# One set of group-norm statistics for both halves of a retention head, applied a few quarter products later

## The chip, the core and the metric

One NeuronCore of a Trainium2 chip runs the whole layer. The engines are PE (TensorE, matmuls and transposes through the array), DVE (VectorE), ACT (ScalarE), POOL (GpSimd) and SP, which here issues the DMAs. The metric is the device time of one execution in microseconds, as a median of several runs; lower is better.

## What is computed

A decoder layer with two groups of eight heads of 128 channels over 1024 tokens: stick-breaking attention in group A, retention in group B. One input projection (2048 to 8192) feeds both and one output projection (2048 to 2048) takes both. Of the reference, what bears on the change:

```python
def head_group_norm(o, gain):
    mu = jnp.mean(o, axis=-1, keepdims=True)
    var = jnp.mean(jnp.square(o - mu), axis=-1, keepdims=True)
    return merge_heads((o - mu) * lax.rsqrt(var + EPS)) * gain.astype(jnp.float32)
...
    qr = rotary(split_heads(q_r, RET_HEADS))
    kr = rotary(split_heads(k_r, RET_HEADS)) * (HEAD_DIM ** -0.5)
    vr = split_heads(v_r, RET_HEADS).astype(jnp.float32)
    ob = head_group_norm(chunkwise_retention(qr, kr, vr), ret_norm_gain[layer])
    ob = ob * jax.nn.silu(z_r.astype(jnp.float32))
    y = jnp.concatenate([oa, ob], axis=-1).astype(x.dtype) @ w_out[layer]
```

`chunkwise_retention` works in eight chunks of 128 tokens: inside a chunk masked scores times values, across chunks a state of 128 x 128 that decays and grows. Each token's 128 outputs of a head are then normalized to mean 0 and variance 1.

## The kernel before

**The large products.** Both projections are matrix products split by a scheme with seven products in place of eight (P1 to P7 per group of 256 output columns). Each product runs four quarters (`j` from 0 to 3), and a quarter is three matmuls of 128x128 by 128x512 (`mm3`, L150 to L152): a weight's high part times a high part, high times low, low times high. In `run` (L357) the order of products in a group's steady state is P1, P4 and P3 of the group before, P6, P7, P2, P5. After each quarter `tick` (L168) runs. The unit of time in this text is therefore the quarter product.

**What a product needs.** For each, `first` (L256) makes the high part `wh` of its weights on ACT and `second` (L262) the low part `wl` on DVE, two products ahead; three buffers of each turn. `make` (L249) forms sums of weights on POOL. Behind products, `copied` (L279) takes a result out of PSUM on ACT, `added` (L290) adds one on DVE, and `copied` lets POOL add an older partial sum six quarters later (L287). Results then pass through rotary tables or a sigmoid (`second_put`, L804: L821 and L824, L841 to L849).

**The heads ride along.** The order on every engine is the program's own. `heads` is a generator: `yield n` lets n quarters go by. `at(k, fn)` (L165) puts work k quarters later; `tick` emits what is due. So an engine meets the work of a head between that of the products, and a waiting instruction holds up everything behind it on its engine.

**A retention head** (`ret_heads`, L1055) has two halves g of four chunks each. With T the quarter at which `values_r(0)` is called:

- at T and T + 6, `values_r(g)` (L1114) issues eight matmuls (seven in the first chunk's half) into `op`, a PSUM bank: A0 for the first half, C for the second. It allocates `on` (a `be` tile) and issues a DMA for `z`.
- one quarter after each, `stats` (L1127): four `bn_stats` on DVE;
- two after, `first_guess` (L1131): four `bn_aggr`, then `m` = variance + EPS and a first `y` for its inverse root;
- three, four and five after, `better` (L1137): one Newton step of three instructions each, on tiles of 128x4; the last also makes `m` = -mean times `y`;
- seven after, that is T + 7 and T + 13, `normal` (L1142): four ACT instructions that write `op` times `y` plus `m` into `on`.
- At T + 12 the next head's values are transposed on PE into banks A1 and B, where that head's inputs are there; ACT copies them to `v` at T + 14 (L755).
- At T + 18 and T + 20, `finish(g)` (L1153) transposes `on` on PE into bank B for the first half and A0 for the second, and one quarter later DVE multiplies by gain and gate (L1159).

In the trace `on` and `kd` are `be`, `pT` is `a`, `st6` is `st`, and q and k of the head are `r`.

## Time and profile before

| | us |
|---|---|
| median of 3 runs | 2088.36 |
| lowest and highest | 2084.07, 2092.07 |
| the profiled execution, whole | 2088.51 |
| its span, first to last instruction | 2086.7 |
| its mean granted PE clock (share of full speed) | 0.978 |
| `bn_stats` of the retention heads, first to last start | 1454.1 to 1827.0 |

A row of the timeline gives start and duration in us from the span's start, the engine, the source line, the operation, output and inputs, shapes, the count of instructions merged, and in brackets how long the engine was idle just before and what released it. A group's row gives the count, then busy us and the mean ns of one, then the idle time before. A row of waits gives who waited for whom, then us in total, times and the longest. Matmuls overlap: one takes 0.4 us from start to end, and the next starts about 0.23 us after it.

### The profile page before, as it was taken

The numbers are of one execution on the slowest core, as the hardware profiler recorded it, in microseconds if no ns is written. First come the engines' busy times: TensorE is split into PE (matmuls) and PEld (weight loads), VectorE is DVE, ScalarE is ACT, GpSimd is POOL, SyncE is SP. The second block draws the span as 40 slices with busy tenths as digits, with TensorE's granted clock in tenths as the row PEclk, the third lists the DMA queues.
The fourth block names the chain that finished last, engine by engine and source line by source line (L and its number), as shares of the span: only waits on it lengthen the run. The fifth ranks groups of instructions, "written<-read, shape, count | busy, mean of one in ns | idle before, by whom it ended". The sixth has DMA issues, their size and how long they took to land. (4 is left out here: it accounts for less than half of the span.)

```text
span 2086.7 us, 27289 instructions
## 1 busy us (share of the span) xinstructions
PE 1961.6 (94%) x9089; PEld 1565.1 (75%) x9089; DVE 1449.8 (69%) x2194; ACT 940.8 (45%) x1718; POOL 919.8 (44%) x627
## 2 busy tenths in 40 slices
PE   5879999998999999999999999899899988998998
PEld 4467777775767777788888888687787876887887
DVE  6678877566668576775766655888687877548555
ACT  4443344544455545554444544454353545335222
POOL 0434577765544335232222322777364654145443
PEclk9879999999999999999999999999999999999999
DMA  9748877533455454544434424777485876447665
GB/s 299 226 130 281 255 231 255 166 106 120 148 162 156 142 148 152 157 142 132 147 126 126 152 97 155 243 237 261 151 273 193 274 249 229 155 164 237 202 192 177
DMA packets 287330, 388.45 MB, mean 186 GB/s; under 512 B 32106, under 2 KB 164276, under 8 KB 287188
## 3 DMA queue, kind: packets, MB, share of 16 engines
q1 hardware_dynamic: 286784, 386.65, 57.4%
q8 instruction: 72, 1.18, 0.2%
q14 instruction: 70, 0.57, 0.1%
q10 hardware_dynamic: 404, 0.05, 0.0%
HBM read 278.51 MB, written 108.10 MB: 185 GB/s over the span
## 5 line engine op out<-in xcount | busy, mean ns | idle before, releaser
L264 DVE TENSOR_TENSOR wl_e_P<-wr_e,wh_e_P 128x512 fp32r<-128x512 f32 x560 | 528.4, 944 | 211.8 <-ACT wh_e_P L259 206.3
L254 POOL TENSOR_TENSOR wr_e<-wr_e,wr_e 128x512 f32<-128x512 f32 x240 | 352.8, 1485 | 494.7 <-DVE wl_e_P L264 441.0
L259 ACT ACTIVATE wh_e_P<-wr_e 128x512 fp32r<-128x512 f32 x560 | 350.1, 628 | 253.1 <-PE b_o L151 23.5
L254 POOL TENSOR_TENSOR wr_e<-wr_e 128x512 f32<-128x512 f32 x80 | 112.9, 1411 | 134.4 <-DVE wl_e_P L264 120.3
L915 DVE TENSOR_TENSOR_SCAN om<-om 128x128 f32<-128x128 f32 (+2 forms) x96 | 119.4, 1243 | 57.0 <-ACT om L906 55.2
L287 POOL TENSOR_TENSOR u_e<-u_e,c_e 128x512 f32<-128x512 f32 x50 | 78.2, 1567 | 119.8 <-DMA c_e<-part 84.5
L287 POOL TENSOR_TENSOR p_e<-p_e,c_e 128x512 f32<-128x512 f32 x49 | 73.5, 1500 | 112.4 <-DMA c_e<-part 70.4
L435 DVE SCALAR_TENSOR_TENSOR acc_b<-ada_b,silu_c,acc_b 128x512 f32<-128x512 f32 x88 | 97.5, 1108 | 29.5 <-DMA ada_b<-in_w_ada_dram 28.8
L152 PE MATMUL b_h<-S_h,wl_e_P 128*128 128x512 f32 x192 | 77.3, 402 | 11.8 <-DVE wl_e_P L264 11.8
L152 PE MATMUL b_e<-S_h,wl_e_P 128*128 128x512 f32 x192 | 77.3, 403 | 8.1 <-DVE wl_e_P L264 8.1
L150 PE MATMUL b_e<-S_h,wh_e_P 128*128 128x512 f32 x192 | 76.8, 400 | 5.7 <-ACT p_e L284 5.7
L921 DVE TENSOR_TENSOR be<-be,om 128x127 f32<-128x127 f32 (+2 forms) x96 | 75.0, 781 | 7.8
L151 PE MATMUL b_h<-S_l,wh_e_P 128*128 128x512 f32 x192 | 76.3, 398 | 2.4 <-DVE S_l L147 1.7
L150 PE MATMUL b_h<-S_h,wh_e_P 128*128 128x512 f32 x192 | 77.9, 406 | 0.0
L962 PE MATMUL oT<-a,v 128*128 128x256 f32 x320 | 76.9, 379 | 0.0
L150 PE MATMUL b_f<-S_h,wh_e_P 128*128 128x512 f32 x192 | 76.5, 398 | 0.0
L151 PE MATMUL b_e<-S_l,wh_e_P 128*128 128x512 f32 x192 | 76.0, 396 | 0.0
L150 PE MATMUL b_g<-S_h,wh_e_P 128*128 128x512 f32 x192 | 75.7, 394 | 0.0
L152 PE MATMUL b_f<-S_h,wl_e_P 128*128 128x512 f32 x192 | 75.1, 391 | 0.4 <-DVE wl_e_P L264 0.4
L151 PE MATMUL b_f<-S_l,wh_e_P 128*128 128x512 f32 x192 | 75.3, 392 | 0.0
L152 PE MATMUL b_g<-S_h,wl_e_P 128*128 128x512 f32 x192 | 75.1, 391 | 0.0
L151 PE MATMUL b_g<-S_l,wh_e_P 128*128 128x512 f32 x192 | 75.0, 391 | 0.0
(487 smaller groups left out, 5532.6 us busy)
## 6 DMA issues: line engine op xcount, KB each, us to landing
wr_e<-in_w_in_dram SPq DMA_DIRECT2D x128, 512.0 KB, 5.2
ada_b<-in_w_ada_dram SPq DMA_DIRECT2D x128, 256.0 KB, 4.8
c_e<-part SPq DMA_DIRECT2D x128, 256.0 KB, 4.9
ada_a<-in_w_ada_dram SPq DMA_DIRECT2D x64, 256.0 KB, 4.5
wr_e<-in_w_out_dram SPq DMA_DIRECT2D x32, 512.0 KB, 4.6
ld<-fin SPq DMA_DIRECT2D x54, 256.0 KB, 4.9
part<-p_e SPq DMA_DIRECT2D x48, 256.0 KB, 4.8
part<-u_e SPq DMA_DIRECT2D x48, 256.0 KB, 2.1
```

What stands on the lines that cost most here:

```text
L150: nc.tensor.matmul(o, a_hi, b_hi, start=first, stop=False, skip_group_check=True)
L151: nc.tensor.matmul(o, a_hi, b_lo, start=False, stop=False, skip_group_check=True)
L152: nc.tensor.matmul(o, a_lo, b_hi, start=False, stop=last, skip_group_check=True)
L254: nc.gpsimd.tensor_tensor(t[o], t[a], t[b], op=op)
L259: nc.scalar.activation(hi, self.t[RIGHT[p]], AF.Copy)
L264: nc.vector.tensor_tensor(lo, self.t[RIGHT[p]], self.parts[p].bitcast(F32), op=ALU.subtract)
L287: at(6, lambda: nc.gpsimd.tensor_tensor(t, t, o, op=ALU.add))
L435: nc.vector.scalar_tensor_tensor(acc, src, cj, acc, op0=ALU.mult, op1=ALU.add)
L915: nc.vector.tensor_tensor_scan(rev, rev, rev, init, op0=ALU.mult, op1=ALU.bypass)
L921: nc.vector.tensor_tensor(be[:, :m], be[:, :m], om[:, 1:m + 1], op=ALU.mult)
L962: nc.tensor.matmul(ob, v[:, j, :], a[:, cl], start=diag and ib == 0 and b == 0 and j2 == 0, stop=ch == 0 and ib == 2, skip_group_check=True)
```

## The change

`first_guess` and `better` are no longer run for each half. `stats` of both halves write into one `st6` of eight blocks. After the second half's `stats`, `first_guess` aggregates all eight, and the inverse root is worked out once on tiles of 128x8. From the second half's call, T + 6, the times are two, three, four and five quarters as before; `normal(0)` comes after eight (T + 14, before: T + 7) and `normal(1)` after ten (T + 16, before: T + 13). Each head's tiles `st6`, `mv`, `m`, `y`, `u` have one buffer of twice the size in place of two.

```diff
-            kds, pTs = {}, {}
+            kds, pTs, ops = {}, {}, {}
+
+            st6 = hs.tile([P, NB, 6], F32, tag="st6", bufs=1, name=f"st6_{h}")
+            mv = hs.tile([P, NB, 2], F32, tag="mv", bufs=1, name=f"mv_{h}")
+            m, y, u = (hs.tile([P, NB], F32, tag=f"{n}4", bufs=1, name=f"{n}4_{h}") for n in "myu")
...
-                st6 = hs.tile([P, 4, 6], F32, tag="st6", bufs=2, name=f"st6_{h}_{g}")
-                mv = hs.tile([P, 4, 2], F32, tag="mv", bufs=2, name=f"mv_{h}_{g}")
-                m, y, u = (hs.tile([P, 4], F32, tag=f"{n}4", bufs=2, name=f"{n}4_{h}_{g}") for n in "myu")
                 on = ht("be", f"on{g}")
+                ops[g] = op, on
 
                 def stats():
                     for j in range(4):
-                        nc.vector.bn_stats(st6[:, j, :], op[:, j, :])
+                        nc.vector.bn_stats(st6[:, 4 * g + j, :], op[:, j, :])
 
                 def first_guess():
-                    for j in range(4):
+                    for j in range(NB):
                         nc.vector.bn_aggr(mv[:, j, :], st6[:, j, :])
...
-                def normal():
+                def normal(g_):
+                    op_, on_ = ops.pop(g_)
                     for j in range(4):
-                        nc.scalar.activation(on[:, j, :], op[:, j, :], AF.Identity, scale=y[:, j:j + 1],
-                                             bias=m[:, j:j + 1])
-                for n, fn in ((1, stats), (2, first_guess), (3, better), (4, better), (5, lambda: better(True)),
-                              (7, normal)):
-                    at(n, fn)
+                        c_ = 4 * g_ + j
+                        nc.scalar.activation(on_[:, j, :], op_[:, j, :], AF.Identity, scale=y[:, c_:c_ + 1],
+                                             bias=m[:, c_:c_ + 1])
+                at(1, stats)
+                if g:
+                    for n, fn in ((2, first_guess), (3, better), (4, better), (5, lambda: better(True)),
+                                  (8, lambda: normal(0)), (10, lambda: normal(1))):
+                        at(n, fn)
```

## The prediction

> **What bounds the kernel now.** First the page's span and busy times.

> ```profile
> span 2086.7 us, 27289 instructions
> PE 1961.6 (94%) x9089; PEld 1565.1 (75%) x9089; DVE 1449.8 (69%) x2194; ACT 940.8 (45%) x1718; POOL 919.8 (44%) x627
> ```

> PE works nearly always, and the change leaves every matmul in place. It can pay only where PE waits, so next I read who waited for whom among 1440 and 1845 us, where the retention heads run.

> ```profile
> PE b_h L152 <- DVE wl_e_P L264: 11.6, 6, 3.0
> PE otp L1156 <- ACT v L755: 5.5, 3, 1.9
> ACT be L1144 <- DVE m L1140: 41.1, 13, 6.0
> ```

> The columns are us in total, times, longest. PE waits for the low parts of weights (`wl`, made on DVE) and, at `finish`, for ACT. ACT itself stands 41.1 us in front of `normal` until DVE has made `m`. The chain of statistics thus holds two engines back, and PE behind them. Where, the busy time by stretch shows: one row a head, 0 to 7, from the first product of `values_r(0)` to the last transpose of `finish(1)` (stretch, its us, busy us of PE, PEld, DVE, ACT, POOL with counts, granted clock, DMA share, GB/s).

> ```profile
> 1449.40:1477.93 28.53, 21.85 (x108) 17.92 (x107) 23.18 (x59) 10.31 (x21) 11.76 (x9) 0.89 0.69 217
> 1500.20:1518.30 18.10, 18.10 (x100) 15.57 (x99) 15.16 (x51) 8.24 (x18) 5.17 (x4) 1.00 0.41 132
> 1555.82:1582.00 26.18, 21.11 (x108) 17.01 (x107) 22.89 (x59) 10.30 (x21) 12.20 (x9) 0.93 0.62 209
> 1604.00:1622.10 18.10, 18.10 (x100) 15.57 (x99) 16.54 (x52) 8.42 (x18) 7.39 (x6) 1.00 0.58 184
> 1659.74:1687.37 27.63, 22.87 (x108) 18.63 (x107) 22.79 (x59) 10.30 (x21) 12.12 (x9) 0.88 0.74 244
> 1709.40:1736.80 27.40, 21.08 (x100) 16.31 (x99) 22.31 (x63) 13.64 (x28) 8.78 (x7) 0.94 0.70 222
> 1777.70:1796.70 19.00, 19.00 (x108) 16.37 (x107) 13.65 (x48) 8.77 (x18) 4.84 (x4) 1.00 0.46 151
> 1818.70:1836.80 18.10, 18.10 (x100) 15.57 (x99) 12.33 (x48) 8.26 (x17) 3.84 (x3) 1.00 0.35 116
> ```

> Heads 0, 2, 4 and 6 issue the same 108 matmuls there (eight transposes of the next head's `v` among them), and head 6 needs 19.00 us without a wait. So heads 0, 2 and 4 lose 9.53 + 7.18 + 8.63 = **25.3 us**. Of the heads with 100 matmuls, 1, 3 and 7 lose nothing against 18.10 and head 5 loses 9.3. Part of each loss is a clock of 0.5 that is granted after the waits, as in head 4:

> ```profile
> 1676.50:1679.90 3.40, 3.40 (x9) 2.67 (x9) 3.02 (x16) 0.37 (x1) 1.56 (x1) 0.50 0.56 176
> ```

> At half speed about half of such a stretch is lost; less the waits inside it I count 1.6 us.

> **What is removed on DVE.** The groups of that stage (busy us, mean ns | idle before):

> ```profile
> L143 DVE SCALAR_TENSOR_TENSOR y<-u,y 128x4 f32<-128x4 f32 x48 | 18.9, 394 | 1.6
> L141 DVE TENSOR_TENSOR u<-y 128x4 f32<-128x4 f32 x48 | 13.1, 273 | 1.2
> L142 DVE SCALAR_TENSOR_TENSOR u<-u,m 128x4 f32<-128x4 f32 x48 | 12.0, 250 | 1.7
> L1134 DVE TENSOR_SCALAR m<-mv 128x4 f32<-128x4 f32 x16 | 5.7, 353 | 0.5
> L139 DVE TENSOR_SCALAR y<-m 128x4 int32<-128x4 int32 x16 | 3.8, 236 | 0.6
> L1140 DVE SCALAR_TENSOR_TENSOR m<-mv,y 128x4 f32<-128x4 f32 x16 | 2.6, 162 | 0.6
> L141 DVE TENSOR_TENSOR nu<-ny x24: 174/176/1134, 541.6 to 878.2; 128x16 f32<-128x16 f32 x24
> ```

> These are 192 instructions, 56.1 us; half go, 12 a head, 96 in all. The others get eight columns: between the 0.16 us of four and the 0.176 us median of sixteen (last row), so at most 96 x 0.015 = 1.4 us more. The saving on DVE is between 96 x 0.16 = 15 us, at the unhindered price, and 28 us, at the mean. The 16 `bn_stats` and `bn_aggr` of a head stay; four `bn_aggr` move into the later chain (0.37 us, below). What this is worth depends on where DVE is late, so I walk through two heads.

> **Heads 0, 2 and 4.** Their order is the same; head 2 from its timeline (start, us):

> ```profile
> 1561.97 0.37 DVE L1133 BATCH_NORM_AGGREGATE mv<-st 128x2 f32<-128x6 f32 x4
> 1565.98 1.24 DVE L141 TENSOR_TENSOR u<-y 128x4 f32<-128x4 f32 x1
> 1567.26 1.20 DVE L142 SCALAR_TENSOR_TENSOR u<-u,m 128x4 f32<-128x4 f32 x1
> 1568.49 1.21 DVE L143 SCALAR_TENSOR_TENSOR y<-u,y 128x4 f32<-128x4 f32 x1
> 1571.81 0.67 DVE L264 TENSOR_TENSOR wl_e_P<-wr_e,wh_e_P 128x512 fp32r<-128x512 f32 x1
> 1576.27 0.16 DVE L1140 SCALAR_TENSOR_TENSOR m<-mv,y 128x4 f32<-128x4 f32 x1
> 1565.54 2.91 POOL L254 TENSOR_TENSOR wr_e<-wr_e,wr_e 128x512 f32<-128x512 f32 x2 [0.70 <-DVE wl_e_P L264]
> 1570.52 1.51 ACT L1144 ACTIVATE be<-op,m,y 128x128 f32<-128x128 f32 x4 [5.98 <-DVE m L1140]
> 1578.37 1.09 ACT L755 ACTIVATE v<-vtp_vT 128x512 f32<-128x512 f32 x2
> 1572.54 0.50 PE L152 MATMUL b_h<-S_h,wl_e_P 128*128 128x512 f32 x1 [2.95 <-DVE wl_e_P L264]
> 1579.52 0.66 PE L1156 MATMUL otp<-ident,be 128*128 128x128 f32 x4 [1.75 <-ACT v L755]
> 1794.28 0.60 PE L1156 MATMUL otp<-ident,be 128*128 128x128 f32 x4
> ```

> The first chain spreads from 1561.97 to 1570.5, where `normal(0)` is released, because POOL is at work and three of its instructions take 1.2 us. `wl` at 1571.81 stands behind it, and PE for 2.95 us. Two full-width instructions of 0.67 us are mixed in; the other 7.2 us go. `wl` can move up to about 1564.6, and this wait of PE is gone. The one chain left has 12 instructions of 0.2 us (0.16, and 6.2 us of idle before 192 of them, 0.03 each), 2.4 us, and eight `bn_aggr`, 0.74 us. Today's second chain ends at 1576.4 and lasts 2.8 us at these prices, so it would begin at 1573.6 - 7.2 = 1566.4 at the earliest; the two full-width instructions ahead of it then meet POOL's burst (two sums of 1.45 us) and may be held up a microsecond each, so 1568.4 at the latest. I take 1567.9, nearer the late end because POOL's burst itself depends on a `wl` and comes earlier too. One instruction of the chain I count as held up, by 1.05 us (1.21 - 0.16). `m` then ends near 1572.1.

> PE's side: head 6 goes from 1777.70 to `finish(0)` at 1794.28, 16.58 us; added to 1555.82 that is 1572.4 unhindered. The next product's `wl` follows `m`: 1572.1 + 0.7 = 1572.8, and PE wants it one matmul (0.2 us) before `finish(0)`, so it is about 0.6 us late (bounds 0 and 2.95, today's wait). ACT has `normal(0)` ahead of the two `v` copies: 1572.1 + 1.51 + 1.09 = 1574.7. `finish(0)` wants bank B, which the second copy frees, at 1573.0: 1.7 us (bounds 0 and 1.75 + 1.51, today's wait and a `normal`). `normal(1)` ends at 1576.2; `finish(1)` comes 1.8 us after `finish(0)` (head 1 below: its stretch ends at 1518.30, its last four transposes take 0.6) and wants it at 1576.5: nothing. So 2.3 us a head remain, and the three gain 25.3 - 6.9 = **18.4 us**.

> **Heads 1 and 3** have no wait today; head 1:

> ```profile
> 1507.61 0.48 PE L150 MATMUL d_h<-A_h,wh_e_P 128*128 128x512 f32 x1
> 1514.26 0.16 DVE L1140 SCALAR_TENSOR_TENSOR m<-mv,y 128x4 f32<-128x4 f32 x1
> 1514.34 0.69 DVE L293 TENSOR_TENSOR c_e<-b_h,c_e 128x512 f32<-128x512 f32 x1
> 1515.07 0.63 ACT L821 ACTIVATE om<-c_e 128x512 f32<-128x512 f32 x1 [3.31 <-DVE c_e L293]
> 1515.61 1.49 ACT L1144 ACTIVATE be<-op,m,y 128x128 f32<-128x128 f32 x4
> 1516.98 0.61 ACT L284 ACTIVATE u_e<-b_h 128x512 f32<-128x512 f32 x1
> 1515.87 0.60 PE L1156 MATMUL otp<-ident,be 128*128 128x128 f32 x4
> ```

> DVE is not behind here (the second half's products end only at 1507.6, first row), so `m` comes no earlier: four more `bn_aggr` make it 0.37 us later. At 1515.61 + 0.37 = 1516.0 ACT starts not `normal(1)` but `normal(0)`, until 1517.5. `finish(0)` wanted it at 1515.87: 1.6 us. Behind it stand a copy and a `wh` (0.5 us each) and `normal(1)`, until 1520.0; `finish(1)`, 1.8 us after `finish(0)`, then waits another 0.6. That is **2.2 us** a head, 4.4 us for two. The lower bound is nothing; the upper adds a half-clock stretch, 3.8 us.

> **The others.** Head 5 is crowded with splits of the second group's operands. Removing a chain takes its DVE lag down by some 2.8 us, but ACT then has both `normal` and the splits ahead of the `finish` pair; I take 0, bounds -3 and +3. Heads 6 and 7 have DVE to spare and ACT just in time: 0, at most +1 each. Bank A0 and a `be` tile are held until `normal(0)`, seven quarter products later, but A0's next writer is `finish(1)`, still later: nothing, and were it sooner, PE would wait as for bank B. One buffer in place of two costs nothing: the next head's statistics begin tens of us after `normal(1)`. No DMA is added or moved.

> **The clock.** Half speed after the new waits: I allow one stretch, 1.6 us (bounds 0 and five). [...]

> **Sum:** -18.4 + 4.4 + 0 + 1.6 = **-12.4 us**. The profiled execution took 2088.5 us around its 2086.7 us span and the median of the runs is 2088.4, so 2076.0.

> **Rivals.**
> *The hold-up is inherited* (0.18). POOL's instructions stay, and each may hold up one more of the chain left, two more than I took: `m` is 2.1 us later and all behind it, so heads 0, 2 and 4 keep 4.4 us, and the gain falls by 6.3 to 6: 2082. For it: 1.24, 1.20, 1.21 in a row under POOL's work. Against: the burst is mostly over when the chain starts. [...]

> *ACT becomes the bound* (0.12). `normal(0)`, `normal(1)` and the `v` copies, 1.51 + 1.51 + 1.09 us, lie in the six quarter products (about 5 us) before `finish(1)`, with two or three more ACT instructions. If `m` falls fully into POOL's burst (4 us late), heads 0, 2 and 4 keep their whole 25.3; heads 1, 3 and 7 pay 3.8 each and head 5 pays 3: +14, 2102. It decides once the waits at `finish` over all heads exceed 25.3 us.

> *Nothing is left to wait for* (0.10): heads 0, 2, 4 run as head 6, the odd heads pay nothing: -25, 2063.

> **How the numbers follow.** My forecast has 0.60, spread over about 2069 to 2083. 2067 to 2090 leaves out the ends, about 2 in 10. A measurement tells 0.5%, 10.4 us, from no change, so faster is below 2077.9: 0.37 of my 0.60 and the 0.10, 0.47. Slower is most of ACT's case, 0.09. The rest, 0.44, is the same.

> **What would show it.** After: no PE wait on `wl` of nearly 3 us in heads 0, 2, 4, those stretches near 21.3 us; the 41.1 us of ACT before `normal` mostly gone; new PE waits at `otp` on ACT `normal` in heads 1 and 3, their stretches near 20.3; the Newton steps (L141 to L143) on 128x8, 24 of each. If the even stretches stay above 25 us, or heads 6 and 7 grow by 2, I am wrong.

## The result and the profile after

The median went from 2087.18 us (6 runs) to 2073.77 us (6 runs, 2070.60 to 2078.84). The ratio is 0.9939, with a 95% interval of 0.9925 to 0.9953: faster by 0.6%, or 13.4 us from median to median. The forecast was 2076.0. The profiled execution took 2072.09 us around this span:

```profile
span 2070.3 us, 27207 instructions
PE 1957.0 (95%) x9089; PEld 1564.0 (76%) x9089; DVE 1427.0 (69%) x2098; ACT 941.0 (45%) x1718; POOL 925.6 (45%) x627
```

DVE has 96 instructions less; the counts of the other engines in this row are as before. Next, where the time went. The same view by stretch as in the prediction, for the changed kernel: one row a head, from the first product of `values_r(0)` to the last transpose of `finish(1)`; the last row is the whole stage, from the first head's `ktp` (the transposes with which a head begins) to the last head's last `finish`.

```profile
1445.70:1470.04 24.34, 20.98 (x108) 17.51 (x107) 21.22 (x47) 10.42 (x21) 13.15 (x9) 0.93 0.72 244
1491.95:1511.47 19.52, 19.41 (x100) 15.58 (x99) 14.53 (x40) 8.46 (x19) 6.75 (x5) 1.00 0.45 146
1547.96:1571.64 23.68, 20.98 (x108) 17.43 (x107) 20.56 (x47) 10.42 (x21) 12.60 (x9) 0.93 0.68 227
1593.69:1613.20 19.51, 19.41 (x100) 15.58 (x99) 14.85 (x41) 8.46 (x19) 6.87 (x6) 1.00 0.50 161
1649.65:1671.54 21.89, 19.47 (x108) 16.30 (x107) 20.15 (x47) 10.43 (x21) 12.46 (x8) 1.00 0.80 269
1693.49:1722.18 28.69, 21.44 (x100) 16.53 (x99) 23.06 (x52) 14.95 (x31) 12.77 (x9) 0.94 0.73 238
1760.92:1779.92 19.00, 19.00 (x108) 16.38 (x107) 9.85 (x36) 8.55 (x18) 4.86 (x4) 1.00 0.51 175
1801.86:1819.95 18.09, 18.09 (x100) 15.55 (x99) 10.45 (x36) 7.46 (x16) 3.84 (x3) 1.00 0.34 117
1425.01:1819.95 394.94, 377.74 (x1944) 315.12 (x1943) 293.84 (x552) 179.70 (x334) 203.76 (x137) 0.99 0.67 224
```

The same stage of the kernel before:

```profile
1428.67:1836.80 408.13, 380.81 (x1944) 317.11 (x1943) 309.54 (x648) 180.01 (x335) 199.53 (x137) 0.97 0.66 217
```

The stage is 13.2 us shorter, nearly what the medians differ by. (These two executions differ by 16.4 us from end to end. The other 3.2 are no gain of the change: the stage begins 3.7 us earlier here, at 1425.0 in place of 1428.7, though both kernels do the same work up to it, and over all profiles below it begins between 1423.5 and 1431.0.) By head: 4.19, 2.50 and 5.74 us gained in the stretches of heads 0, 2 and 4 (12.4 together), 1.42, 1.41 and 1.29 lost in those of heads 1, 3 and 5, nothing in 6 and 7. That is 8.3 us; the other 4.9 lie between the stretches, mainly behind heads 1, 3 and 5.

Who waited for whom in the changed kernel (us in total, times, longest):

```profile
ACT be L1148 <- DVE m L1142: 11.7, 4, 4.0
PE b_h L152 <- DVE wl_e_P L264: 6.0, 4, 2.0
PE otp L1162 <- ACT v L755: 4.1, 3, 1.4
PE otp L1162 <- ACT be L1148: 3.1, 1, 3.1
```

ACT waits 11.7 us for `m`, before 41.1. PE's waits on `wl` in `b_h` went from 11.6 to 6.0 us, those at `finish` on the `v` copies from 5.5 to 4.1. The 3.1 us are in head 5.

How far the waits were removed, and why not all of them, the timeline of head 0 shows (T is 1445.70):

```profile
1451.70 1.61 DVE L264 TENSOR_TENSOR wl_e_P<-wr_e,wh_e_P 128x512 fp32r<-128x512 f32 x1
1453.84 1.79 DVE L846 TENSOR_TENSOR c_e<-c_e,om 128x512 f32<-128x512 f32 x1
1457.24 1.77 DVE L849 TENSOR_TENSOR c_e<-c_e,ld 128x512 f32<-128x512 f32 x1
1458.94 0.63 DVE L1135 BATCH_NORM_AGGREGATE mv<-st 128x2 f32<-128x6 f32 x8
...
1461.64 1.25 DVE L141 TENSOR_TENSOR u<-y 128x8 f32<-128x8 f32 x1
...
1463.33 0.17 DVE L1142 SCALAR_TENSOR_TENSOR m<-mv,y 128x8 f32<-128x8 f32 x1
1463.43 0.69 DVE L264 TENSOR_TENSOR wl_e_P<-wr_e,wh_e_P 128x512 fp32r<-128x512 f32 x1
1455.04 3.43 POOL L254 TENSOR_TENSOR wr_e<-wr_e,wr_e 128x512 f32<-128x512 f32 x2
1463.53 1.50 ACT L1148 ACTIVATE be<-op,m,y 128x128 f32<-128x128 f32 x4 [3.98 <-DVE m L1142]
1464.18 0.50 PE L152 MATMUL b_h<-A_h,wl_e_P 128*128 128x512 f32 x1 [1.98 <-DVE wl_e_P L264]
1466.06 1.11 PE L1162 MATMUL otp<-ident,be 128*128 128x128 f32 x4 [1.38 <-ACT v L755]
```

The reader is to see three things. The wait of nearly 3 us in the middle of the product is gone; of PE's waits only those at the end are left, 1.98 us for the `wl` behind `m` and 1.38 us for bank B. The chain begins at T + 13.2 (T + 12.7 and T + 12.3 in heads 2 and 4), not at T + 12.1 as forecast, because three of the full-width instructions ahead of it now take 1.6 to 1.8 us each (0.67 unhindered) while POOL works: the hold-up has changed places. (In the stage of both kernels a `wl` that runs beside no POOL instruction takes at most 0.69 us; of the 43 before and 54 after that run beside one, the median takes about 1.18 us and the longest 1.80.) In the chain itself one instruction is held up to 1.25 us, as forecast, and the one behind the aggregations (L1136) takes 0.60 us (0.58 to 0.60 in the three heads), which was not forecast. `m` ends at T + 17.8 (in heads 2 and 4 at T + 17.1 and T + 16.8), where T + 16.3 was forecast.

The Newton steps on DVE in the changed kernel:

```profile
L143 DVE SCALAR_TENSOR_TENSOR y<-u,y 128x8 f32<-128x8 f32 x24 | 7.9, 330 | 0.8
L141 DVE TENSOR_TENSOR u<-y 128x8 f32<-128x8 f32 x24 | 7.1, 295 | 0.5
L142 DVE SCALAR_TENSOR_TENSOR u<-u,m 128x8 f32<-128x8 f32 x24 | 4.0, 167 | 0.8
L1136 DVE TENSOR_SCALAR m<-mv 128x8 f32<-128x8 f32 x8 | 2.6, 329 | 0.3
L139 DVE TENSOR_SCALAR y<-m 128x8 int32<-128x8 int32 x8 | 2.4, 302 | 0.3
L1142 DVE SCALAR_TENSOR_TENSOR m<-mv,y 128x8 f32<-128x8 f32 x8 | 1.3, 167 | 0.3
```

These groups sum to 25.3 us; those of before summed to 56.1. They lost 30.8 us, but DVE as a whole lost only 309.54 - 293.84 = 15.7 in the stage. The other 15.1 us went to the instructions that stayed. About half of that shows in the 107 low parts `wl` of the stage, before and after:

```profile
L264 DVE TENSOR_TENSOR wl_e_P<-wr_e,wh_e_P 128x512 fp32r<-128x512 f32 x107 | 96.0, 897 | 20.2 <-ACT wh_e_P L259 20.2
L264 DVE TENSOR_TENSOR wl_e_P<-wr_e,wh_e_P 128x512 fp32r<-128x512 f32 x107 | 103.1, 963 | 23.8 <-ACT wh_e_P L259 23.7
```

Most of the rest is in the twelve rotary products that write `c_e` (L846, L849), 20.2 us in place of 13.0. These are the instructions that the timeline of head 0 shows at 1.6 to 1.8 us while POOL works.

### The profile page after: what moved, and what is told of

It is laid out like the page before. It is cut to its first block, busy times and chain, and to the rows that moved or that the text cites. A ratio compares the mean times of both kernels' runs of the same rounds, so it can differ in the third digit from the quotient of the medians.

```text
span 2070.3 us, 27207 instructions
## 1 busy us (share of the span) xinstructions
PE 1957.0 (95%) x9089; PEld 1564.0 (76%) x9089; DVE 1427.0 (69%) x2098; ACT 941.0 (45%) x1718; POOL 925.6 (45%) x627
## 3 DMA queue, kind: packets, MB, share of 16 engines
q8 instruction: 72, 1.18, 0.2%
## 5 line engine op out<-in xcount | busy, mean ns | idle before, releaser
L264 DVE TENSOR_TENSOR wl_e_P<-wr_e,wh_e_P 128x512 fp32r<-128x512 f32 x560 | 528.9, 945 | 218.1 <-ACT wh_e_P L259 213.1
L254 POOL TENSOR_TENSOR wr_e<-wr_e,wr_e 128x512 f32<-128x512 f32 x240 | 354.6, 1492 | 495.3 <-DVE wl_e_P L264 445.7
L259 ACT ACTIVATE wh_e_P<-wr_e 128x512 fp32r<-128x512 f32 x560 | 350.7, 628 | 276.1 <-PE b_o L151 28.1
L254 POOL TENSOR_TENSOR wr_e<-wr_e 128x512 f32<-128x512 f32 x80 | 112.9, 1411 | 134.5 <-DVE wl_e_P L264 120.3
L435 DVE SCALAR_TENSOR_TENSOR acc_b<-ada_b,silu_c,acc_b 128x512 f32<-128x512 f32 x88 | 97.3, 1106 | 27.4 <-DMA ada_b<-in_w_ada_dram 26.9
L152 PE MATMUL b_e<-S_h,wl_e_P 128*128 128x512 f32 x192 | 77.6, 404 | 7.9 <-DVE wl_e_P L264 7.7
L150 PE MATMUL b_e<-S_h,wh_e_P 128*128 128x512 f32 x192 | 77.1, 401 | 5.7 <-ACT p_e L284 5.7
L152 PE MATMUL b_h<-S_h,wl_e_P 128*128 128x512 f32 x192 | 75.7, 394 | 4.2 <-DVE wl_e_P L264 4.2
L150 PE MATMUL b_h<-S_h,wh_e_P 128*128 128x512 f32 x192 | 76.7, 400 | 0.0
L150 PE MATMUL b_f<-S_h,wh_e_P 128*128 128x512 f32 x192 | 76.3, 398 | 0.0
L150 PE MATMUL b_g<-S_h,wh_e_P 128*128 128x512 f32 x192 | 75.8, 395 | 0.0
L152 PE MATMUL b_f<-S_h,wl_e_P 128*128 128x512 f32 x192 | 74.9, 390 | 0.4 <-DVE wl_e_P L264 0.4
L152 PE MATMUL b_g<-S_h,wl_e_P 128*128 128x512 f32 x192 | 74.9, 390 | 0.0
```

Source lines behind the costliest of these rows:

```text
L150: nc.tensor.matmul(o, a_hi, b_hi, start=first, stop=False, skip_group_check=True)
L152: nc.tensor.matmul(o, a_lo, b_hi, start=False, stop=last, skip_group_check=True)
L254: nc.gpsimd.tensor_tensor(t[o], t[a], t[b], op=op)
L259: nc.scalar.activation(hi, self.t[RIGHT[p]], AF.Copy)
L264: nc.vector.tensor_tensor(lo, self.t[RIGHT[p]], self.parts[p].bitcast(F32), op=ALU.subtract)
L435: nc.vector.scalar_tensor_tensor(acc, src, cj, acc, op0=ALU.mult, op1=ALU.add)
```

## The experiments

Four questions: which part of the change brings the gain (its two parts are one chain in place of two, and the later `normal`); why PE still waits; whether it is DVE's time ahead of `wl` that matters; and what the held-up instructions add. "Stage" is the stage row as above, of one profiled execution each, which need not be a typical one: that of v_copies_sooner took 5.3 us less than the median of its runs, that of two_chains_late_normal 4.8 more. The stretches are those of heads 0 to 5 (heads 6 and 7 stayed within 0.1 us throughout, but for head 7 of twelve_free, 1.1 longer). "Half" counts the stretches of 3.41 us in the stage at a granted clock of half speed.

| kernel | median us | ratio to before (interval) | stage us | stretches of heads 0 to 5 | half |
|---|---|---|---|---|---|
| before | 2087.18 | | 408.1 | 28.5 18.1 26.2 18.1 27.6 27.4 | 6 |
| changed | 2073.77 | 0.9939 (0.9925 to 0.9953) | 394.9 | 24.3 19.5 23.7 19.5 21.9 28.7 | 3 |
| two_chains_late_normal | 2079.32 | 0.9972 (0.9960 to 0.9985) | 400.7 | 24.5 19.7 23.6 19.2 24.9 31.6 | 5 |
| one_chain_early_normal | 2082.79 | 0.9981 (0.9971 to 0.9991) | 405.4 | 26.3 18.1 27.0 18.1 26.6 26.4 | 8 |
| v_copies_sooner | 2069.27 | 0.9911 (0.9891 to 0.9931) | 389.5 | 23.1 19.5 20.9 19.5 20.4 29.1 | 3 |
| before_v_ahead | 2079.20 | 0.9963 (0.9946 to 0.9980) | 398.7 | 24.3 18.1 23.7 18.1 23.8 30.1 | 5 |
| wl_before_last_step | 2077.08 | 0.9954 (0.9939 to 0.9969) | 399.3 | 25.9 19.0 25.3 19.0 26.2 26.3 | 5 |
| v_turned_sooner | 2070.46 | 0.9915 (0.9891 to 0.9938) | 392.5 | 21.5 18.1 23.3 18.1 21.5 28.1 | 2 |
| no_newton | 2059.43 | 0.9859 (0.9836 to 0.9881) | 381.5 | 19.8 18.1 20.3 18.1 20.9 27.3 | 1 |
| v_sooner_two_newton | 2061.13 | 0.9879 (0.9856 to 0.9903) | 384.4 | 19.9 19.1 20.0 19.1 19.9 29.3 | 1 |
| twelve_held | 2088.01 | 1.0002 (0.9991 to 1.0013) | 406.9 | 27.6 19.6 25.8 19.5 26.5 31.2 | 7 |
| twelve_free | 2092.73 | 1.0027 (1.0015 to 1.0039) | 414.0 | 26.8 22.1 25.3 22.1 26.5 32.5 | 9 |
| changed_again | 2075.14 | 0.9948 (0.9932 to 0.9964) | 397.1 | 25.1 19.5 22.4 19.5 23.8 28.7 | 5 |

### One part of the change at a time

**two_chains_late_normal** is the kernel before with only the times of `normal` changed (to T + 14 and T + 16):

```diff
                 for n, fn in ((1, stats), (2, first_guess), (3, better), (4, better), (5, lambda: better(True)),
-                              (7, normal)):
+                              (10 if g else 14, normal)):
```

> The kernel before with both chains of statistics left as they were and only the two normals moved to T + 14 and T + 16, as in the change. My theory: heads 0, 2 and 4 were slow because the first chain stands on DVE ahead of the low parts of weights (wl); ACT's wait in front of normal cost nothing by itself. Then PE's waits on wl of nearly 3 us in heads 0, 2 and 4 stay, the waits at finish come on top, and the time is 2086 to 2094. Rival: the change won because ACT no longer stands 41 us in front of normal with weights queued behind it. Then the waits on wl go without any instruction of DVE being removed, and the time is 2073 to 2079.

Head 2's timeline:

```profile
1568.16 1.50 ACT L1144 ACTIVATE be<-op,m,y 128x128 f32<-128x128 f32 x4
1569.54 1.09 ACT L755 ACTIVATE v<-vtp_vT 128x512 f32<-128x512 f32 x2
1570.18 0.52 PE L152 MATMUL b_h<-S_h,wl_e_P 128*128 128x512 f32 x1 [2.03 <-DVE wl_e_P L264]
```

The waits on `wl` stayed, 11.4 us against 11.6, as both chains still run. But no wait at `finish` on the `v` copies appears at all in heads 0, 2 and 4, where the kernel before has 5.5 us. The rows show why: before, the copies stood on ACT behind a `normal(1)` that waited for the second chain's `m`; here `normal(0)` and the copies go first, and `normal(0)` need not wait: its `m` is there at 1568.12 in this head, 0.04 us before ACT comes to it. In heads 1 and 3 the later `normal` costs 1.1 to 1.6 us, as in the changed kernel. So the later `normal` is worth 0.28% by itself, and PE's waits put that down to what it lets past on ACT. Neither theory had that.

**one_chain_early_normal** is the changed kernel with `normal` at the earliest times (T + 12 and T + 13):

```diff
                     for n, fn in ((2, first_guess), (3, better), (4, better), (5, lambda: better(True)),
-                                  (8, lambda: normal(0)), (10, lambda: normal(1))):
+                                  (6, lambda: normal(0)), (7, lambda: normal(1))):
```

> The changed kernel with normal(0) and normal(1) at T + 12 and T + 13, right behind the chain, not at T + 14 and T + 16. My theory: heads 1 and 3 lose their waits at finish (1.4 us each), while in heads 0, 2 and 4 the v copies now stand behind both normals and bank B is freed 1.5 to 2 us later: -3 and +5, so 2074 to 2079. Rival: the later time is what makes the gain (ACT must not stand in front of normal); then ACT's wait before normal is back, PE's waits on wl with it, and the time is above 2081.

Its head 0:

```profile
1465.63 2.90 ACT L1148 ACTIVATE be<-op,m,y 128x128 f32<-128x128 f32 x8 [5.85 <-DVE m L1142]
1468.90 1.12 ACT L755 ACTIVATE v<-vtp_vT 128x512 f32<-128x512 f32 x2
1470.08 1.11 PE L1162 MATMUL otp<-ident,be 128*128 128x128 f32 x4 [3.00 <-ACT v L755]
```

Both `normal` (2.90 us) now stand between `m` and the copies, and PE waits 3.0 to 3.3 us for bank B in each even head. Heads 1 and 3 are back at 18.1. The wait for bank B is longer by 1.6 to 1.9 us, as forecast, but the time lies above the forecast, where the rival had it. The waits on `wl` explain little of that: they are 2.23, 2.16 and 1.79 us in heads 0, 2 and 4, where the changed kernel has 1.98, 1.32 and 1.04. What the forecast left out is the clock: eight half-clock stretches, where the two profiles of the changed kernel have three and five, so 5 to 8.5 us more at an estimated 1.7 us (half of 3.41) each. The two parts alone bring 0.28% and 0.19%, together 0.61% (0.52% when the changed kernel was run again): about additive.

**before_v_ahead** is the kernel before with nothing changed on DVE; only ACT's two copies go one quarter earlier, to T + 13, and `normal(1)` one later, to T + 14:

```diff
-    def turn_v(raw, v, hf, tag):
+    def turn_v(raw, v, hf, tag, k=2):
...
-        at(2, lambda: nc.scalar.activation(v[:, 4 * hf:4 * hf + 4], tp, AF.Copy))
+        at(k, lambda: nc.scalar.activation(v[:, 4 * hf:4 * hf + 4], tp, AF.Copy))
...
-            turn_v(vts[hf], v, hf, ("A1", "B")[hf])
+            turn_v(vts[hf], v, hf, ("A1", "B")[hf], 1)
...
-                              (7, normal)):
+                              (8 if g else 7, normal)):
```

> The kernel before with one thing changed on ACT: the v copies at T + 13 and normal(1) at T + 14, so the copies stand ahead of normal(1), which waits for m. Both chains of statistics and normal(0) at T + 7 stay. My theory by now: the gain of the change has two parts, DVE's time ahead of wl and the v copies no longer queued behind the last m. Then PE's waits at finish (1.89, 1.75, 1.89 us) go and those on wl stay: 5.5 us and one or two half-clock stretches of 1.6, so 2077 to 2081. Rival: the waits at finish only hide that wl and m are late; then other waits take their place, and the time is 2083 to 2088.

```profile
1564.31 0.50 PE L152 MATMUL b_h<-S_h,wl_e_P 128*128 128x512 f32 x1 [2.54 <-DVE wl_e_P L264]
1564.67 1.10 ACT L755 ACTIVATE v<-vtp_vT 128x512 f32<-128x512 f32 x2
1568.25 1.50 ACT L1144 ACTIVATE be<-op,m,y 128x128 f32<-128x128 f32 x4 [1.95 <-DVE m L1140]
1569.24 0.60 PE L1156 MATMUL otp<-ident,be 128*128 128x128 f32 x4
```

In this timeline (head 2) the copies run while ACT would otherwise wait, and `finish(0)` waits for nothing. The `wl` waits stay (2.54 us here). The time is within the forecast. By 0.37%, two copies ahead of a waiting instruction are worth over half of what the change brings, by another way (the change itself removes most of the waits on `wl` and leaves those at `finish`), and heads 1 and 3 pay nothing for it.

### Why PE still waits in the changed kernel

**v_copies_sooner** is the changed kernel with the same edit of `turn_v` (`normal` as changed).

> The changed kernel with the two v copies one quarter product sooner, at T + 13, ahead of normal(0) on ACT. My theory: in heads 0, 2 and 4 finish(0) waits 1.38 us for bank B, which the v copies free behind normal(0); ACT is idle for 3 to 4 us in front of normal(0), so the copies fit there, and the wait falls by about 1.2 us a head: 2068 to 2072. Rival: finish(0) waits for m and normal(0) as much as for the copies; then the wait has another name and the time stays at 2072 to 2076.

The waits at `finish` on the copies are gone, and the even stretches are shorter by 1.3 to 2.8 us; left is the wait on `wl`, 1.98, 1.36 and 0.86 us in heads 0, 2, 4. So the 1.38 us a head were the copies behind `normal(0)`, as the prediction had it.

**wl_before_last_step** puts the last Newton step behind the `wl` for which PE waits:

```diff
-                    for n, fn in ((2, first_guess), (3, better), (4, better), (5, lambda: better(True)),
+                    for n, fn in ((2, first_guess), (3, better), (4, better), (6, lambda: better(True)),
```

> The changed kernel with the last Newton step one quarter later, behind the wl that PE waits for (1.98, 1.32 and 1.04 us in heads 0, 2 and 4). My theory: wl comes 0.8 us sooner (four instructions of 0.2 us) but m 0.6 us later, and finish(0) waits for what comes behind m: 2071 to 2076, one wait traded for another. Rival: the wait on wl is a loss of its own; then three heads gain 0.8 us each and a half-clock stretch or two goes: 2066 to 2071.

PE's waits (us in total, times, longest):

```profile
PE otp L1162 <- ACT v L755: 12.1, 3, 4.8
```

The wait was traded and grew: `wl` is late by less than 1 us, but `m` ends 1.5 to 2.2 us later, with `normal(0)` and the copies behind it, and PE waits 3.6 to 4.8 us at `finish`. Both expectations were too good.

**v_turned_sooner** has the edit of `turn_v` as well, and transposes `v` two quarters earlier, so that copies and both `normal` come sooner:

```diff
-            yield RT_GAP
+            yield RT_GAP - 2
...
-            yield RT_GAP
+            yield RT_GAP + 2
             finish(0, *o0)
...
-                                  (8, lambda: normal(0)), (10, lambda: normal(1))):
+                                  (6, lambda: normal(0)), (8, lambda: normal(1))):
```

> The changed kernel with the next head's v turned at T + 10 and copied at T + 11, normal(0) at T + 12 and normal(1) at T + 14. My theory: with the copies out of the way, early normals cost nothing in heads 0, 2 and 4 (as in v_copies_sooner, about 21.5 us on average), and in heads 1 and 3 normal(0) is no longer behind the sigmoid of c_e: 18.1 and not 19.5 us. 2064 to 2069. Rival: what one_chain_early_normal lost, it lost by ACT standing before normal with weights behind it; then the time is 2074 or more.

PE's waits:

```profile
PE vtp_vT L754 <- DMA vT<-fin: 2.7, 3, 1.4
```

Heads 1 and 3 are at 18.1 again, so what they pay in the changed kernel is `normal(0)` being late. But now PE waits for the DMA that brings the next head's `v`, 1.45 and 1.05 us behind heads 1 and 3: the transposes cannot go earlier for nothing. And its waits on `wl` are longer in heads 2 and 4, 2.22 and 1.85 us. The time is 2070.5, slightly above the forecast.

### Is it DVE's time ahead of `wl`?

**no_newton** leaves out the three Newton steps, nine DVE instructions a head; its output is normalized with the first guess alone and is off by some 2%, so it serves to measure time only. (`better` then makes only `m`.)

> The changed kernel without its three Newton steps (the first guess of y is used as it is), nine instructions of DVE fewer a head, all else at its time. My theory: what is left in heads 0, 2 and 4 is the one chain ahead of wl, and in heads 1 and 3 the chain ahead of c_e, the sigmoid and normal(0). With it gone the stretches of heads 0, 2 and 4 fall from 24.3, 23.7 and 21.9 to 19 to 20.5 us and of heads 1 and 3 from 19.5 to 18.1: 2056 to 2064. Rival: POOL's hold-ups pass on to full-width instructions of DVE, wl stays late, and the time is 2067 to 2074.

No wait on `wl` is left in heads 0 to 4, at 2059.4 us; what is left there are 0.60, 1.08 and 1.39 us at `finish` for the copies. **v_sooner_two_newton** combines v_copies_sooner with two Newton steps in place of three:

```diff
-                    for n, fn in ((2, first_guess), (3, better), (4, better), (5, lambda: better(True)),
+                    for n, fn in ((2, first_guess), (3, better), (5, lambda: better(True)),
```

> v_copies_sooner with two Newton steps in place of three (one step is left out; the error of y after two is some parts in a million). My theory: three instructions fewer ahead of wl and of m, 0.6 us and at times a hold-up of 1.05: the waits on wl in heads 0, 2 and 4 (1.98, 1.36, 0.86) fall by 0.6 to 1.6, the odd heads by 0.6: 2064 to 2068. Rival: no difference to v_copies_sooner, 2069.

The wait on `wl` falls to 0.3 to 0.4 us in heads 0, 2, 4, the even stretches to 19.9 or 20.0 and the time to 2061.1, below the forecast and 12 us below the changed kernel. Three DVE instructions a head less took 0.5 to 1.7 us of wait from a head, and two half-clock stretches with it.

**twelve_held** adds to the changed kernel twelve DVE products in the place of the first half's chain, of a tile with itself that nothing else reads:

```diff
+                def extra():
+                    for _ in range(3):
+                        nc.vector.tensor_tensor(dz, dz, dz, op=ALU.mult)
+                if not g:
+                    for n in (2, 3, 4, 5):
+                        at(n, extra)
```

> The changed kernel with 12 extra DVE instructions a head where the first chain stood (T + 2 to T + 5): 128x4 products of a tile with itself, two inputs from SBUF as the Newton steps have, that nothing waits for. Unhindered 12 x 0.2 = 2.4 us. My theory: the chain removed was dear because its instructions are held up by POOL's; then these cost heads 0, 2 and 4 a good part of what the change won there, their stretches are 26 to 28 us (24.3, 23.7 and 21.9 without), and the time is 2080 to 2087. Rival: POOL holds up some instruction of DVE anyway, so it is their own 2.4 us and no more: the same time as twelve_free within 3 us.

The group of the added products (busy us, mean ns | idle before), then those of head 0:

```profile
L1156 DVE TENSOR_TENSOR dz<-dz 128x4 f32<-128x4 f32 x96 | 34.1, 356 | 2.9
```

```profile
1457.16 3.09 DVE L1156 TENSOR_TENSOR dz<-dz 128x4 f32<-128x4 f32 x6
1461.37 4.32 DVE L1156 TENSOR_TENSOR dz<-dz 128x4 f32<-128x4 f32 x6
```

The ratio is 1.0002: the whole gain is given back, though `normal` still comes late (2088.0, 1 us above the forecast). The mid-product waits are back too (2.65 and 2.93 us in heads 0 and 2). Two parts of that can be told apart. The twelve instructions take DVE time again, 34.1 us over the stage against the 30.8 that the change removed, and bring back the waits on `wl`, which two_chains_late_normal has too (0.9972). The other 0.3% come on top, as far as the waits show, because here `normal(0)` waits for an `m` that is late, and the copies with it: the 1.37 us at `finish` in each even head, which two_chains_late_normal does not have.

**twelve_free** was to add the same DVE time by instructions that no row of the kernel before shows held up, 24 `bn_aggr` (six at a time in place of three; the 64 of that kernel took 0.14 to 0.17 us each, also the 20 beside POOL's work):

```diff
+                    for _ in range(6):
+                        nc.vector.bn_aggr(dz[:, 0:2], st6[:, 0, :])
```

> As twelve_held, but the extra instructions are 24 aggregations of 128x6 into 128x2 (0.09 us each in a row, 2.2 us together), a form that was never held up in the trace before (174 ns at most). My theory: most of 2.2 us fits into the time in which DVE waits there, stretches of heads 0, 2 and 4 grow by 0 to 2 us: 2074 to 2080, at least 4 us below twelve_held. Rival: within 3 us of twelve_held.

```profile
L1156 DVE BATCH_NORM_AGGREGATE dz<-st 128x2 f32<-128x6 f32 x192 | 34.8, 181 | 6.2
```

The price was wrong: written into one tile they take (34.8 + 6.2) / 192 = 0.21 us each, 5.1 us a head, not 0.09 each. So the comparison is not at the same price, and 2092.7 meets neither theory. In heads 1 and 3, where POOL is busy for 7.2 and 7.8 us (11.1 to 11.8 in the even heads), that is 5.1 us against some 2.4 for the held products (12 x 0.2), and the stretches are 2.5 and 2.6 us longer: PE waits 1.66 and 1.67 us at `finish` there, and a half-clock stretch follows each. In the even heads the held products took 3.09 + 4.32 = 7.4 us of DVE (head 0), 2.3 more than the free ones, and yet the stretches differ by less than 0.9. That would fit hold-ups that pass from the instruction that is gone to the next one, so that removing held instructions saves about their own unhindered time. But it is one comparison at unequal sizes, and DVE's total does not tell the two kinds apart: in the stage it rises by 19.8 us (to 313.64) with the held products, whose rows sum to 34.1, and by 23.1 (to 316.96) with the free ones, whose rows sum to 34.8. Either way the instructions that were there before take less: a `wl` 918 and 942 ns in the mean, in the changed kernel 963. The 15.1 us of the first section are the better evidence.

**changed_again** is the changed kernel once more, to see how far one profile can be trusted.

> The changed kernel itself, once more on the same chip as the two others: 2071 to 2076 by every theory; the stretches of heads 0, 2 and 4 at 22 to 24.5 us if the readings of the first profile are typical.

The median is within the forecast. The even stretches, however, are 25.1, 22.4 and 23.8 where the first profile has 24.3, 23.7 and 21.9: a difference of 1 to 2 us in a single stretch says nothing, as five half-clock stretches fell into this execution and three into the first. Behind the same waits (within 0.5 us each) the clock fell in another place.

## Why the prediction was right, point by point

**What bounds it.** Right: PE's waits in heads 0, 2, 4, and the change touches nothing else. The waits themselves went from 16.5 us (2.83, 1.95 and 1.89 in head 0, 2.95, 0.37 and 1.75 in head 2, 2.87 and 1.89 in head 4) to 3 x 1.38 + 1.98 + 1.32 + 1.04 = 8.5.

**DVE's saving.** Forecast 15 to 28 us; measured 15.7, near the unhindered price: 96 x 0.161 us less 96 x 0.006 for the wider tiles (167 ns for eight columns, 161 for four), 14.9.

**The even heads.** -18.4 forecast, -12.4 measured. The mechanism was right: no `wl` wait in mid-product, one behind `m`, one for bank B, nothing at `finish(1)`. The step that was mis-sized is the place of the chain: "I take 1567.9", T + 12.1. The full-width instructions ahead of it, in head 0 held up by 0.9 to 1.1 us in three cases, put it at T + 13.2 there and at T + 12.7 and T + 12.3 in heads 2 and 4. The chain itself takes 4.5 us where 4.2 were reckoned, as its L1136 takes 0.6 us too. So `wl` is 1.0 to 2.0 us late in place of 0.6. The wait for bank B, 1.7 forecast, was 1.38. Together 8.5 us of waits remain where 6.9 were forecast; two half-clock stretches, an estimated 1.7 us each, are most of the rest.

**Heads 1 and 3.** +4.4 forecast, +2.8 measured. The term priced a whole `normal` behind which `finish(0)` starts. The rows of head 1 show something else:

```profile
1505.85 0.17 DVE L1142 SCALAR_TENSOR_TENSOR m<-mv,y 128x8 f32<-128x8 f32 x1
1507.19 1.49 ACT L1148 ACTIVATE be<-op,m,y 128x128 f32<-128x128 f32 x4
1507.69 1.38 PE L1162 MATMUL otp<-ident,be 128*128 128x128 f32 x4
1510.29 1.18 PE L1162 MATMUL otp<-ident,be 128*128 128x128 f32 x4
```

Each of the four transposes starts when its own of the four ACT instructions ends, 0.05 us later for the first half. They spread to 1.38 and 1.18 us where they take 0.60 unhindered: 0.78 + 0.58 = 1.36 of the 1.42 lost, and the forecast wait of a whole `normal` did not appear among the waits. Nor did `m` come 0.37 later: it ended at T + 14.07, before at T + 14.22. And the lost time came partly back: from `ktp` to `ktp` heads 1 and 3 are only 0.39 and 0.23 us longer, since in the kernel before PE then waited 0.55 and 0.69 us for the DMA of the next `v`, and now does not. The prediction's sum left out everything between the stretches.

**Head 5.** 0 forecast; its stretch is 1.3 us longer, its whole interval 0.9 shorter. Within the bounds. ACT does have `normal` and the splits ahead of `finish`, as written: PE waits 3.1 us there. Why its stretch moves about from kernel to kernel (26 to 32 us in the table) stays open.

**Heads 6 and 7** did not change, and one buffer in place of two and the longer hold on bank A0 cost nothing visible: right.

**The clock.** One half-clock stretch allowed, three measured (two of them in heads 0 and 2), against six before. In the sum the prediction priced the clock together with the waits that it follows. In head 4 of the kernel before, the stretch from 1683.28 follows a wait of 1.89 us at `finish(0)`; in it matmuls of 512 columns start 0.43 us apart, at full speed 0.23. So about half of its 3.41 us is lost, and at an estimated 1.7 us each, three fewer are 5.1 of the 13.2 us; in the second profile one fewer, 1.7 of 11.0. Without them the stage gains 8.1 and 9.3 us.

**The sum** held because mis-sized terms offset. Even heads with their clock 4.4 us worse than forecast (-12.4 against -18.4 + 1.6), odd heads 1.6 better, head 5 1.3 worse, and 4.9 gained between the stretches: -12.4 + 4.4 - 1.6 + 1.3 - 4.9 = -13.2. That the total came within about 1 us is luck: the term for the even heads alone was 4.4 us off, and the stage of the changed kernel differs by some 2 us between its own two profiles.

**The rivals.** "The hold-up is inherited" was half right: instructions ahead of the chain inherited it, not the chain, where one was held as taken. It cost less than its 2.1 us a head. "ACT becomes the bound" did not happen, but one_chain_early_normal shows the way to it: with both `normal` ahead of the copies ACT gave back two thirds of the gain. "Nothing left to wait for" is nearly v_sooner_two_newton. **What the prediction lacked** is that a good half of the gain can be had from ACT's order alone: it saw `normal(0)` ahead of the copies in the new order, but not that the wait for bank B in the old order came from a `normal(1)` ahead of them.

## What to carry to other kernels

Before shortening a late chain, look at what stands behind the instruction that waits for it: moving two ready copies ahead of the waiting one brought 0.37% here, over half of the 0.61% of the whole change. Where instructions are held up beside another engine's work, do not count a removed one at its held-up time: here 30.8 us of them were worth 15.7, about their unhindered time. And waits of 1 to 2 us cost more than their length here where two of them fell into the same 3.41 us: 2.9 us of waits in head 0 were followed by a half-clock stretch, an estimated 1.7 us more.

## What was not expected of the hardware

```profile
1462.48:1465.90 3.42, 0.50 (x1) 0.19 (x1) 3.32 (x7) 2.37 (x7) 1.66 (x2) 1.00 0.10 35
1465.90:1469.31 3.41, 3.25 (x10) 2.76 (x11) 2.23 (x4) 2.02 (x6) 0.00 (x0) 0.50 0.94 300
1663.87:1667.28 3.41, 2.37 (x12) 1.64 (x10) 3.07 (x13) 0.76 (x3) 0.59 (x2) 1.00 0.90 293
1667.28:1670.69 3.41, 2.03 (x10) 1.52 (x11) 3.15 (x4) 3.41 (x10) 1.26 (x1) 1.00 0.52 152
1670.69:1674.10 3.41, 3.41 (x20) 2.85 (x19) 1.52 (x3) 2.05 (x5) 0.00 (x0) 1.00 0.94 313
```

In head 0 both waits fall into one cell, 2.9 us idle, and the next cell runs at half speed. In head 4 a cell boundary parts the waits, 1.04 us and 1.38 us, and neither cell is followed by one at half speed. That would also fit the changed kernel's stretches, which differ between its two profiles with three and five cells at half speed. It is a reading of traces; no kernel was made to shift the grid. In the kernel before, 2.1 us of waits in one cell (from 1468.24) were enough; of its cells with less, 1.83 us (from 1679.87) were followed by half speed and 1.92 us (from 1737.89) were not.

**Aggregations into the same columns took longer.** `bn_aggr` into eight different columns took 0.08 us each (0.63 for eight, head 0), into the same columns 0.21 (twelve_free), about the 0.20 from one dependent Newton instruction to the next. What makes the difference was not tested.
